# Block one's gates and branch projections turned token-major, and the last gate superblock moved ahead of the queries

## The chip, the core and the metric

One core of a Trainium2 chip runs the whole program once. The metric is device microseconds of that launch, lower is better. The core has a matrix engine (TensorE, PE in the rows, with its weight loads as PEld), VectorE (DVE), ScalarE (ACT), GpSimdE (POOL) and the queue engine SyncE (SP) that issues most DMAs.

## What is computed

Two transformer blocks over 256 tokens of width 2048, all in float32. The change lies in the first block, in this part of it:

```python
mod = (c @ w_mod + b_mod).reshape(B, 6, D)           # six rows of 2048
h = rms_norm(x, g_pre_mix) * (1 + scale_m) + shift_m
proj = h @ w_in                                       # uv, q latent, k, v, index, two gates of 2048
y_a = gmlp_spatial_gating(proj[uv], ...)              # 256 x 1024
y_b = dsa_attention(q, k, v, ...)                     # 256 x 1024, 8 heads, top-64 keys by an indexer
gates = sigmoid(proj[gate])
merged = gates[..., :D] * (y_a @ w_proj_a) + gates[..., D:] * (y_b @ w_proj_b)
x = x + gate_m * rms_norm(merged @ w_out, g_post_mix)
```

A feed-forward block and a second block (pooling, then dilated attention) follow.

## The kernel before

**Arithmetic.** Every matmul is made of three: each operand is split into a high part rounded for TensorE and a low rest, and high by high, high by low and low by high are summed in PSUM. Weights stream from HBM in pieces of 1 MB (one "call", 4 chunks of 128 rows by 512 columns). `stream_` (lines 126 to 136) loads a piece into one of 3 `raw` buffers and splits it in two halves: ScalarE writes `wh` (L134), VectorE writes `wl` (L135), 3 buffers each.

**Three ways to multiply a superblock of 512 output columns.** `lin` (L149, its matmuls L144 to L146) holds the weights still, 128 columns at a time, and moves the 256 tokens past them: 12 matmuls of 256 columns for a chunk of 128 rows. The result has features on the partitions. `linA` (L174, L192 to L194) and `linT` (L197, L211 to L213) hold 128 tokens still and move the 512 weight columns: 6 matmuls of 512 columns for the same chunk. The result has tokens on the partitions. The last chunk group of `linT` is run token half by token half, so that the first bank is done early; its `mid` is called after the first group.

**Where the low parts lie.** The program shifts the start of a low tile by 32 columns or not. The operands of the later `linT` stages (F, Y, Z) are made with the argument 0, and `xo`, which `linT` reads, with `[:, 32:]`; the operands of `lin` stages (A, K, Q, `ybl`, `yal`) are made with 32, and block one's own `xl` without a shift. K feeds both `lin` (keys) and `linA` (values).

**Order of block one.** `start` normalises the input and runs the first three quarters of rows of the eleven superblocks 0 to 10 of `w_in` (0 q latent; 1, 2 the token-major z; 3, 4 u; 5, 6 keys; 7, 8 token-major values; 9, 10 the first half of the first gate), setting partial sums aside in SBUF. Then jobs follow in the order of the string ORDER: `m` finishes uv, `G2` and `G3` are whole superblocks of the first gate (`gate_all`, 16 chunks), `g9 g10` finish the two begun ones, `k`, `v` keys and values, `S` the spatial gating (`gmlp`, mostly VectorE), `Q` the queries with their rotation (L350 to L352), `A` starts the attention, and `p0` to `p3` multiply y_a by `w_pa` (`proj`, L624: gate times projection into `mrg`). The last loop (L664) takes four superblocks of the second gate (`w_in_g2`) with y_b times `w_pb`, adds into `mrg`, and 16 splits (L680) make the operand `xh`, `xo` of the output projection (`w_out`, by `linT`).

**Side work.** At each weight piece, `side` (L520) emits `rate` tiles of `w_mod` (0.5 MB each, buffers `rawm`, accumulated on VectorE at L460; 96 of them, flushed to `mods` by 16 small matmuls at L442 every 16 tiles) and `pace` steps of a generator. The commands `r3` and `r4` in ORDER set the rate; it is 0 before. After `A` the generator is `attn1` (L1018), one step for one head: scores (L1024) to PSUM, mask, maximum, exponent, scaling, three transposes (L1054), value product (L1030 to L1032), copy into `yb` (L1033). When all heads are out, `yb` is split in two halves of four heads into `ybh` and `ybl` (L336, L337), which the second gate's `w_pb` stage reads. The framework then orders each engine's queue once, by priority and readiness; weight streams have a higher priority.

Of the kernel before, what the change touches and what calls it, by code (L numbers as in the profile page):

```python
# [10 lines left out]
F32R = mybir.dt.float32r  # L11
AF = mybir.ActivationFunctionType
ALU = mybir.AluOpType
# [3 lines left out]
P = 128  # L17
T = 256
D = 2048
KC = D // P  # L20
TX = T + 2
# [7 lines left out]
SCALE = 128.0 ** -0.5  # L29


ORDER = "m2 m3 m4 G2 g9 g10 k0 k1 v7 v8 S r3 Q A r4 p0 p1 p2 G3 p3"

PACE = (3, 1)

# [25 lines left out]
def view(tile, k, t):  # L61

    return tile[:, :k * t].rearrange("p (k t) -> p k t", k=k)
# [26 lines left out]
class Kern:  # L90
# [380 lines left out]
    def block1(self, c1):  # L471
        nc, tc, A = self.nc, self.tc, self.A
        p1 = c1.enter_context(tc.tile_pool(name="p1", bufs=1))
        xh = view(p1.tile([P, KC * TX], F32R, name="xh", tag="xh", bufs=1), KC, T)

        low = lambda i, name, dtype=F32R, t=T, pool=p1: view(
            pool.tile([P, 4 * TX + 56], dtype, name="%s%d" % (name, i), tag="xl%d" % i, bufs=1), 4, t)
        xs = [low(i, "x", F32) for i in range(4)]
        xl = {}
        X = lambda k: (xh[:, k], xl[k // 4][:, k % 4])  # L480
# [6 lines left out]
            if a >= NKEPT:  # L487
                self.cst[k] = cst[:, a - NKEPT:b - NKEPT]
        X8 = lambda name: self.cp.tile([P, 8, T], F32, name=name, tag="x", bufs=2)
        mrg = Halves([X8("mrg0"), None])  # L490
        ql = p1.tile([P, 1024], F32, name="ql", tag="ws", bufs=1)

        sbs = [(False, [ql[:, 0:512], ql[:, 512:1024]])]
# [1 line left out]
        sbs += [(False, [flat(u, 2 * s), flat(u, 2 * s + 1)]) for s in range(2)]  # L495
        sbs += [(False, [flat(kT, 2 * s), flat(kT, 2 * s + 1)]) for s in range(2)]
        sbs += [(True, [v[:, h, s * 512:(s + 1) * 512] for h in range(2)]) for s in range(2)]
        sbs += [(False, [mrg.flat(4 * s), mrg.flat(4 * s + 2)]) for s in range(2)]

# [6 lines left out]
        p1e, p1 = p1, c1.enter_context(tc.tile_pool(name="p1r", bufs=1))  # L506
# [23 lines left out]
        def finish():  # L530
            for _ in self.work:
                pass
# [4 lines left out]
            return (self.linA if tok else self.lin)(A["w_in"], n, X, 4, 4, 512, banks=self.reload(src), k0=12)  # L537

        YH = lambda name: self.place(2, name, F32R, 0)
        YL = lambda name: self.place(3, name, F32R, 32)  # L540
        qlh = p1.tile([P, 4, T], F32R, name="qlh")
        qll = view(p1.tile([P, 1088], F32R, name="qll")[:, 32:], 4, T)
        ssq = self.stat_new()
        for i, bank in enumerate(last(0)):
            for q in range(2):
                k = 2 * i + q
# [39 lines left out]
        for s in range(2):  # L586
            for i, bank in enumerate(self.lin(A["w_qidx"], s, QX, 4, 4, 512)):
                a = self.sp.tile([P, 512], F32, name="qa", tag="sw", bufs=3)
                b = self.sp.tile([P, 512], F32, name="qb", tag="th", bufs=2)
# [13 lines left out]
                nc.scalar.activation(dst, bank, AF.Tanh, scale=0.5)  # L603

        def gate_all(s):
            if mrg.tiles[1] is None:
                mrg.tiles[1] = X8("mrg1")
            for i, bank in enumerate(self.lin(A["w_in"], 9 + s, X, KC, 4, 512)):
                nc.scalar.activation(mrg.flat(4 * s + 2 * i), bank, AF.Tanh, scale=0.5)

        def keys(s):
            dst = sbs[5 + s][1]
# [6 lines left out]
                nc.scalar.copy(dst, bank)  # L619

        def proj(s):
            for i, bank in enumerate(self.lin(A["w_pa"], s, YA, 8, 4, 512)):
                m = mrg.flat(4 * s + 2 * i)
                nc.vector.scalar_tensor_tensor(m, m, 1.0, bank, ALU.add, ALU.mult)  # L624

        ya = []
        YA = lambda k: (ya[0][:, k], ya[1][:, k])

        def spatial():
# [3 lines left out]
            finish()  # L633
            ya.extend([YH("yah"), YL("yal")])
            self.gmlp(p1, u, z, *ya)
# [22 lines left out]
        finish()  # L658
        ybh, ybl = YH("ybh"), YL("ybl")
        YB = lambda k: (ybh[:, k], ybl[:, k])  # L660
        for i in range(2):
            b4 = lambda t: t[:, 4 * i:4 * i + 4]
            self.split(b4(ybh), b4(ybl), b4(yb))
        for s in range(4):  # L664
            gt = []
            for bank in self.lin(A["w_in_g2"], s, X, KC, 4, 512):
                g = self.sp.tile([P, 512], F32, name="gt", tag="gt", bufs=2)
                nc.scalar.activation(g, bank, AF.Tanh, scale=0.5)
                gt.append(g)
            for i, bank in enumerate(self.lin(A["w_pb"], s, YB, 8, 4, 512)):  # L670
                t = self.sp.tile([P, 512], F32, name="mt", tag="th", bufs=2)
                nc.vector.scalar_tensor_tensor(t, gt[i], 1.0, bank, ALU.add, ALU.mult)
                m = mrg.flat(4 * s + 2 * i)
                nc.vector.tensor_add(m, m, t)

        xo = [view(p1e.tile([P, 4 * TX + 56], F32R, name="xo%d" % i, tag="xl%d" % i, bufs=1)[:, 32:], 4, T)
              for i in range(4)]
# [41 lines left out]
        for h in range(2):  # L719
            update(h)  # L720
            self.rsum(r, ss, h)
            for c in range(4):

                m = mix[h][:, c * 512:(c + 1) * 512]
                nc.scalar.activation(m, self.xt[h][:, c * 512:(c + 1) * 512], AF.Copy, scale=r[:, h:h + 1])
                if c < 2:
                    bank = self.acc("b")
# [3 lines left out]
                    for b in range(4):  # L731
                        s = slice(b * P, (b + 1) * P)
                        modulated(4 * c + b, slice(h * P, (h + 1) * P), bank[:, s], tmp[:, s])
        for k in range(8, KC, 2):
            bank = self.acc("b")
            tmp = self.sp.tile([P, 512], F32, name="tm", tag="th", bufs=2)
            for b in range(2):
# [3 lines left out]
                s = slice(b * T, (b + 1) * T)  # L741
# [731 lines left out]
```

## Time and profile before

| | |
|---|---|
| median of 3 runs | 2440.88 us (2440.26 to 2445.6) |
| the profiled execution | 2438.1 us, of which its span in the profile 2436.1 us |
| TensorE busy | 2378.1 us, 98% of the span |
| VectorE, ScalarE busy | 1678.5 us (69%), 1246.7 us (51%) |
| DMA | 540.61 MB, mean 222 GB/s |

Busy shares are means over very different stages. Read the stage that the change touches (about 240 to 690 us) by windows of time, and take durations there from start to start of successive instructions, since matmuls overlap.

### The profile page before, as it was taken

To read this page: it belongs to the slowest core of one execution; us is meant where nothing else is said; L and a number is where in the kernel's file an instruction comes from. 1 tells how busy PE (TensorE), PEld (TensorE's weight loads), DVE (VectorE), ACT (ScalarE), POOL (GpSimd) and SP (SyncE) were. 2 spreads that over 40 slices of the span, in tenths; PEclk is the share of its full clock that TensorE was granted. 3 is DMA by queue.
4 is the path that set the end of the run, shared out by engine and by line. 5 is a ranking of instruction groups with operands and counts; after the bars stand their busy time and mean duration, and the time that the engine had idled before them with its cause. 6 is when DMAs were issued, how large, how long until landed. Compare 5 with 4: busy or idle time off the path is not lost.

```text
span 2436.1 us, 37172 instructions
## 1 busy us (share of the span) xinstructions
PE 2378.1 (98%) x15142; PEld 2153.9 (88%) x15142; DVE 1678.5 (69%) x2213; ACT 1246.7 (51%) x1716; POOL 19.3 (1%) x30
## 2 busy tenths in 40 slices
PE   7999999999989999999999989999999999999997
PEld 6899989999868888888888879998898899999986
DVE  8997898888777575555556566756664477777764
ACT  5877674534464444444445454445644455554543
POOL 0000000000000000000000000000000000000000
PEclk9999999999999999999999999999999999999999
DMA  9997557999948585555555545555655544454453
GB/s 365 349 365 259 182 177 272 329 350 333 350 161 321 191 291 193 190 189 187 194 197 200 190 149 191 191 189 186 228 193 190 190 163 167 158 189 169 161 190 138
DMA packets 104043, 540.61 MB, mean 222 GB/s; under 512 B 9888, under 2 KB 18240, under 8 KB 53184
## 3 DMA queue, kind: packets, MB, share of 16 engines
q1 hardware_dynamic: 100896, 526.19, 60.8%
q10 hardware_dynamic: 2160, 8.88, 1.0%
q0 software_dynamic: 816, 3.16, 0.4%
q8 instruction: 118, 1.93, 0.3%
q14 instruction: 53, 0.43, 0.1%
HBM read 533.99 MB, written 4.21 MB: 221 GB/s over the span
## 4 chain that ended last, share of the span: by engine, by line
PE 94%; DVE 2%; ACT 1%; DMA 1%; issue 1%; POOL 0%; SPq 0%; DVEq 0%; POOLq 0%
PE acca L145 15%; PE acca L144 15%; PE acca L146 15%; PE acca L212 11%; PE acca L211 11%; PE acca L213 11%; PE acca L193 2%; PE acca L194 2%; PE acca L192 2%; PE accb L212 2%; PE accb L213 2%; PE accb L211 2%; DMA hid<-in_w_mod_dram 1%; DVE wl L135 1%; PE accb L1343 1%
## 5 line engine op out<-in xcount | busy, mean ns | idle before, releaser
L135 DVE TENSOR_TENSOR wl<-raw,wh 128x1024 fp32r<-128x1024 f32 x802 | 977.9, 1221 | 570.9 <-ACT wh L134 568.3
L134 ACT CAST wh<-raw 128x1024 fp32r<-128x1024 f32 x802 | 841.7, 1051 | 864.0 <-PE acca L213 377.9
L145 PE MATMUL acca<-Ql,wh 128*128 128x256 f32 x1024 | 290.5, 284 | 0.0
L144 PE MATMUL acca<-Qh,wh 128*128 128x256 f32 x1024 | 289.8, 284 | 0.0
L146 PE MATMUL acca<-Qh,wl 128*128 128x256 f32 x1024 | 285.5, 281 | 0.0
L212 PE MATMUL acca<-wl,Fh 128*128 128x512 f32 x704 | 276.8, 393 | 1.0 <-DVE wl L135 0.9
L213 PE MATMUL acca<-wh,Fl 128*128 128x512 f32 x704 | 275.7, 393 | 0.3 <-DVE Fl L716 0.3
L211 PE MATMUL acca<-wh,Fh 128*128 128x512 f32 x704 | 252.3, 396 | 1.7 <-ACT Fh L714 1.7
L144 PE MATMUL acca<-xh,wh 128*128 128x256 f32 x832 | 232.8, 284 | 4.5 <-ACT xh L808 3.4
L145 PE MATMUL acca<-xl,wh 128*128 128x256 f32 x832 | 233.7, 284 | 0.0
L146 PE MATMUL acca<-xh,wl 128*128 128x256 f32 x832 | 227.0, 283 | 0.0
L144 PEld LDWEIGHTS acca<-Qh,wh 128*128 128x128 f32 x1024 | 192.9, 188 | 0.5
L145 PEld LDWEIGHTS acca<-Ql,wh 128*128 128x128 f32 x1024 | 192.6, 188 | 0.8
L146 PEld LDWEIGHTS acca<-Qh,wl 128*128 128x128 f32 x1024 | 192.1, 189 | 0.4
L144 PEld LDWEIGHTS acca<-xh,wh 128*128 128x128 f32 x832 | 158.1, 190 | 7.3 <-ACT xh L808 3.6
L145 PEld LDWEIGHTS acca<-xl,wh 128*128 128x128 f32 x832 | 157.4, 189 | 1.6 <-issue 0.7
L212 PEld LDWEIGHTS acca<-wl,Fh 128*128 128x128 f32 x704 | 132.7, 189 | 29.1 <-DVE wl L135 2.2
L211 PEld LDWEIGHTS acca<-wh,Fh 128*128 128x128 f32 x704 | 131.3, 188 | 30.0 <-ACT Fh L714 2.9
L213 PEld LDWEIGHTS acca<-wh,Fl 128*128 128x128 f32 x704 | 132.4, 188 | 28.6 <-DVE Fl L716 1.5
L146 PEld LDWEIGHTS acca<-xh,wl 128*128 128x128 f32 x832 | 155.1, 190 | 1.3 <-issue 1.0
L145 PE MATMUL acca<-Al,wh 128*128 128x256 f32 x512 | 143.7, 282 | 0.0
L144 PE MATMUL acca<-Ah,wh 128*128 128x256 f32 x512 | 142.7, 281 | 0.0
(374 smaller groups left out, 4600.5 us busy)
## 6 DMA issues: line engine op xcount, KB each, us to landing
raw<-in_w_fgu_dram SPq DMA_DIRECT2D x88, 1024.0 KB, 4.8
raw<-in_w_inb_dram SPq DMA_DIRECT2D x64, 1024.0 KB, 4.8
raw<-in_w_in_dram SPq DMA_DIRECT2D x51, 1024.0 KB, 6.3
rawm<-in_w_mod_dram SPq DMA_DIRECT2D x96, 512.0 KB, 5.7
raw<-in_w_fd_dram SPq DMA_DIRECT2D x44, 1024.0 KB, 4.8
raw<-in_w_ina_dram SPq DMA_DIRECT2D x32, 1024.0 KB, 4.8
raws<-in_w_mod_dram SPq DMA_DIRECT2D x30, 1024.0 KB, 8.4
raw<-in_w_in_g_dram SPq DMA_DIRECT2D x16, 1024.0 KB, 7.2
```

Source lines behind the costliest of these rows:

```text
L134: nc.scalar.copy(wh[:, :per], raw[:, a:a + per])
L135: nc.vector.tensor_sub(wl[:, :per], raw[:, a:a + per], wh[:, :per].bitcast(F32))
L144: mm(out, ah, bh, start=start, stop=False, skip_group_check=True)
L145: mm(out, ah, bl, start=False, stop=False, skip_group_check=True)
L146: mm(out, al, bh, start=False, stop=stop, skip_group_check=True)
L192: mm(banks[h], xh[:, t], wh[:, s], start=fresh and k == 0, stop=False, skip_group_check=True)
L193: mm(banks[h], xh[:, t], wl[:, s], start=False, stop=False, skip_group_check=True)
L194: mm(banks[h], xl[:, t], wh[:, s], start=False, stop=k == nk - 1, skip_group_check=True)
L211: mm(banks[h][q], xh[:, t], wh[:, w], start=k == 0, stop=False, skip_group_check=True)
L212: mm(banks[h][q], xh[:, t], wl[:, w], start=False, stop=False, skip_group_check=True)
L213: mm(banks[h][q], xl[:, t], wh[:, w], start=False, stop=k == nk - 1, skip_group_check=True)
L1343: nc.tensor.matmul(ps[:, g * T:(g + 1) * T], q[g][:, P:T], kT, start=g == 0, stop=g == 1, skip_group_check=True)
```

## The change

Superblocks 9 and 10 (both their begun and their last part), `G2`, `G3`, the four `p` projections, and the second gate with its `w_pb` products go from `lin` to the token-major `linA` and `linT`. `mrg` becomes two token-half tiles of 2048 columns, both reserved at the start. The operand of the output projection has to be feature-major, so `turn` transposes `mrg` on TensorE, two chunks at a time, and splits from PSUM: six turns inside the last `w_pb` superblock (for the columns of the first three), two behind it. The low tiles `xs`, `xl` move by 32 columns, `yal`/`ybl` change their shift. In ORDER, `G3` goes from between `p2` and `p3` to between `S` and `r3 Q`.

```diff
-ORDER = "m2 m3 m4 G2 g9 g10 k0 k1 v7 v8 S r3 Q A r4 p0 p1 p2 G3 p3"
+ORDER = "m2 m3 m4 G2 g9 g10 k0 k1 v7 v8 S G3 r3 Q A r4 p0 p1 p2 p3"
...
-            pool.tile([P, 4 * TX + 56], dtype, name="%s%d" % (name, i), tag="xl%d" % i, bufs=1), 4, t)
+            pool.tile([P, 4 * TX + 56], dtype, name="%s%d" % (name, i), tag="xl%d" % i, bufs=1)[:, 32:], 4, t)
...
-        mrg = Halves([X8("mrg0"), None])
+        mrg = [X8("mrg%d" % h).rearrange("p a t -> p (a t)") for h in range(2)]
...
-        sbs += [(False, [mrg.flat(4 * s), mrg.flat(4 * s + 2)]) for s in range(2)]
+        sbs += [(True, [m[:, s * 512:(s + 1) * 512] for m in mrg]) for s in range(2)]
...
-        YL = lambda name: self.place(3, name, F32R, 32)
+        YL = lambda name: self.place(3, name, F32R, 0)
...
         def gate_all(s):
...
-            for i, bank in enumerate(self.lin(A["w_in"], 9 + s, X, KC, 4, 512)):
-                nc.scalar.activation(mrg.flat(4 * s + 2 * i), bank, AF.Tanh, scale=0.5)
+            for m, bank in zip(mrg, self.linT(A["w_in"], 9 + s, X, KC, 4, 512)):
+                nc.scalar.activation(m[:, s * 512:(s + 1) * 512], bank[0], AF.Tanh, scale=0.5)
...
         def proj(s):
-            for i, bank in enumerate(self.lin(A["w_pa"], s, YA, 8, 4, 512)):
...
+            for m, bank in zip(mrg, self.linT(A["w_pa"], s, YA, 8, 4, 512)):
...
+        def turn(k):
+            bank = self.acc("b")
+            for b in range(2):
+                for h in range(2):
+                    nc.tensor.transpose(bank[:, b * T + h * P:b * T + (h + 1) * P],
+                                        mrg[h][:, (k + b) * P:(k + b + 1) * P], self.ident)
+            self.split(xh[:, k:k + 2], xo[k // 4][:, k % 4:k % 4 + 2], bank.rearrange("p (b t) -> p b t", b=2), 0.5)
+
         for s in range(4):
             gt = []
-            for bank in self.lin(A["w_in_g2"], s, X, KC, 4, 512):
+            for bank in self.linT(A["w_in_g2"], s, X, KC, 4, 512):
...
-            for i, bank in enumerate(self.lin(A["w_pb"], s, YB, 8, 4, 512)):
+            turned = lambda: [turn(k) for k in (range(0, 12, 2) if s == 3 else ())]
+            banks = self.linT(A["w_pb"], s, YB, 8, 4, 512, mid=turned)
...
+        for k in range(12, 16, 2):
+            turn(k)
         XO = lambda k: (xh[:, k], xo[k // 4][:, k % 4])
-        for k in range(KC):
-            self.split(*XO(k), mrg(k), 0.5)
```

## Rows read from the trace of the kernel before

**Rows 1.** The page: busy time by engine, the chain's shares, the weight split's group.
```profile
PE 2378.1 (98%) x15142; PEld 2153.9 (88%) x15142; DVE 1678.5 (69%) x2213; ACT 1246.7 (51%) x1716; POOL 19.3 (1%) x30
...
PE 94%; DVE 2%; ACT 1%; DMA 1%; issue 1%; POOL 0%; SPq 0%; DVEq 0%; POOLq 0%
...
L135 DVE TENSOR_TENSOR wl<-raw,wh 128x1024 fp32r<-128x1024 f32 x802 | 977.9, 1221 | 570.9 <-ACT wh L134 568.3
```

**Rows 2.** Windows of 20 us: window, length, engines' busy time, PE clock, DMA.
```profile
340.00:360.00 20.00, 20.00 (x141) 18.57 (x140) 19.32 (x35) 13.43 (x21) 0.00 (x0) 1.00 0.47 168
...
500.00:520.00 20.00, 20.00 (x171) 20.00 (x171) 14.99 (x14) 8.45 (x9) 0.00 (x0) 1.00 0.96 352
...
600.00:620.00 20.00, 20.00 (x99) 16.85 (x98) 14.83 (x18) 8.67 (x13) 0.66 (x1) 1.00 0.95 360
```

**Rows 3.** Windows of 1 us in the gap, same columns.
```profile
363.00:364.00 1.00, 0.00 (x0) 0.00 (x0) 1.00 (x2) 1.00 (x2) 0.00 (x0) 1.00 0.81 246
...
367.00:368.00 1.00, 0.00 (x0) 0.00 (x0) 1.00 (x2) 0.53 (x1) 0.00 (x0) 0.53 0.99 377
...
373.00:374.00 1.00, 1.00 (x7) 1.00 (x7) 1.00 (x3) 0.99 (x2) 0.00 (x0) 0.56 0.81 115
```

**Rows 4.** Waits between 330 and 380 us: total us, times, longest.
```profile
PE acca L144 <- DVE qT L350: 6.7, 1, 6.7
```

**Rows 5.** Timeline of PE, a `lin` stage (second gate): start, duration.
```profile
500.49 0.28 PE L144 MATMUL acca<-xh,wh 128*128 128x256 f32 x1
...
507.93 0.28 PE L144 MATMUL acca<-xh,wh 128*128 128x256 f32 x1
```

**Rows 6.** Timeline of PE, a `linT` stage (output projection).
```profile
640.36 0.39 PE L211 MATMUL acca<-wh,xh 128*128 128x512 f32 x1
...
645.80 0.39 PE L211 MATMUL acca<-wh,xh 128*128 128x512 f32 x1
```

**Rows 7.** Timeline of PE, a `linA` stage (values of block two, operand K).
```profile
1860.88 0.39 PE L192 MATMUL acca<-wh,Kh 128*128 128x512 f32 x1
...
1866.43 0.39 PE L192 MATMUL acca<-wh,Kh 128*128 128x512 f32 x1
```

**Rows 8.** Timeline of PE, transposes between matmuls of a `linT` stage.
```profile
1706.63 0.39 PE L213 MATMUL acca<-wh,Yl 128*128 128x512 f32 x1
1706.87 0.38 PE L241 MATMUL accb<-cst,x 128*128 128x128 f32 x2
1707.00 0.48 PE L211 MATMUL acca<-wh,Yh 128*128 128x512 f32 x1
1707.32 0.81 PE L241 MATMUL accb<-cst,x 128*128 128x128 f32 x6
1707.89 0.47 PE L212 MATMUL acca<-wl,Yh 128*128 128x512 f32 x1
1708.20 0.39 PE L213 MATMUL acca<-wh,Yl 128*128 128x512 f32 x1
```

**Rows 9.** Timeline of PE, steps of the attention heads 1, 6, 7 and 8.
```profile
388.65 0.27 PE L1054 MATMUL accb<-cst,e 128*128 128x128 f32 x1
...
441.26 0.27 PE L1054 MATMUL accb<-cst,e 128*128 128x128 f32 x1
...
447.86 0.90 PE L1024 MATMUL accb<-kT,qT 128*128 128x128 f32 x4
...
454.33 0.27 PE L1054 MATMUL accb<-cst,e 128*128 128x128 f32 x1
...
468.19 0.27 PE L1054 MATMUL accb<-cst,e 128*128 128x128 f32 x1
```

**Rows 10.** Instructions by tile: count, duration min/median/max, first and last start.
```profile
L144 PE MATMUL acca<-yah,wh x128: 274/280/551, 369.4 to 453.0; 128*128 128x256 f32 x128
...
L337 DVE TENSOR_TENSOR ybl<-yb,ybh x2: 1211/1214/1218, 458.5 to 474.4; 128x1024 fp32r<-128x1024 f32 x2
...
L144 PE MATMUL acca<-ybh,wh x128: 274/282/367, 478.8 to 595.8; 128*128 128x256 f32 x128
```

More of the change, by code (lines that the diff above doesn't have):

```diff
@@ L605, in gate_all @@
         def gate_all(s):
-            if mrg.tiles[1] is None:
-                mrg.tiles[1] = X8("mrg1")
-            for i, bank in enumerate(self.lin(A["w_in"], 9 + s, X, KC, 4, 512)):
-                nc.scalar.activation(mrg.flat(4 * s + 2 * i), bank, AF.Tanh, scale=0.5)
+            for m, bank in zip(mrg, self.linT(A["w_in"], 9 + s, X, KC, 4, 512)):
+                nc.scalar.activation(m[:, s * 512:(s + 1) * 512], bank[0], AF.Tanh, scale=0.5)
         def keys(s):
@@ L621, in proj @@
         def proj(s):
-            for i, bank in enumerate(self.lin(A["w_pa"], s, YA, 8, 4, 512)):
-                m = mrg.flat(4 * s + 2 * i)
-                nc.vector.scalar_tensor_tensor(m, m, 1.0, bank, ALU.add, ALU.mult)
+            for m, bank in zip(mrg, self.linT(A["w_pa"], s, YA, 8, 4, 512)):
+                m = m[:, s * 512:(s + 1) * 512]
+                nc.vector.scalar_tensor_tensor(m, m, 1.0, bank[0], ALU.add, ALU.mult)
         ya = []
@@ L663, in block1 @@
             self.split(b4(ybh), b4(ybl), b4(yb))
+        def turn(k):
[5 more added lines that the diff above has]
+            self.split(xh[:, k:k + 2], xo[k // 4][:, k % 4:k % 4 + 2], bank.rearrange("p (b t) -> p b t", b=2), 0.5)
         for s in range(4):
             gt = []
-            for bank in self.lin(A["w_in_g2"], s, X, KC, 4, 512):
+            for bank in self.linT(A["w_in_g2"], s, X, KC, 4, 512):
                 g = self.sp.tile([P, 512], F32, name="gt", tag="gt", bufs=2)
-                nc.scalar.activation(g, bank, AF.Tanh, scale=0.5)
+                nc.scalar.activation(g, bank[0], AF.Tanh, scale=0.5)
                 gt.append(g)
-            for i, bank in enumerate(self.lin(A["w_pb"], s, YB, 8, 4, 512)):
+            if s == 3:
+                xo = [view(p1e.tile([P, 4 * TX + 56], F32R, name="xo%d" % i, tag="xl%d" % i, bufs=1)[:, 32:], 4, T)
+                      for i in range(4)]
+            turned = lambda: [turn(k) for k in (range(0, 12, 2) if s == 3 else ())]
+            banks = self.linT(A["w_pb"], s, YB, 8, 4, 512, mid=turned)
+            for h, (m, bank) in enumerate(zip(mrg, banks)):
                 t = self.sp.tile([P, 512], F32, name="mt", tag="th", bufs=2)
-                nc.vector.scalar_tensor_tensor(t, gt[i], 1.0, bank, ALU.add, ALU.mult)
-                m = mrg.flat(4 * s + 2 * i)
+                nc.vector.scalar_tensor_tensor(t, gt[h], 1.0, bank[0], ALU.add, ALU.mult)
+                m = m[:, s * 512:(s + 1) * 512]
                 nc.vector.tensor_add(m, m, t)
-        xo = [view(p1e.tile([P, 4 * TX + 56], F32R, name="xo%d" % i, tag="xl%d" % i, bufs=1)[:, 32:], 4, T)
-              for i in range(4)]
+        for k in range(12, 16, 2):
+            turn(k)
         XO = lambda k: (xh[:, k], xo[k // 4][:, k % 4])
-        for k in range(KC):
-            self.split(*XO(k), mrg(k), 0.5)
         if todo and todo[0][0] < 48:
```

## The prediction

> **What bounds the kernel now.** I read the page first. TensorE is busy for 98% of the span and holds 94% of the chain that ended last [rows 1]. So the time is TensorE's work plus its few holes, and an edit pays only where it shortens TensorE's stream or fills a hole. Windows of time come next. Where the change is, TensorE is full, with VectorE at 15 us or more of 20 and, later on, the DMA share at 0.95 [rows 2]. The exception is a hole from 362.7 us on: VectorE is busy all the time, TensorE does nothing, and its clock, 2.4 GHz until then, drops to half (1.2 GHz) at about 367.5 us and comes back at about 373.6 us [rows 3]. The waits name what ended it: the first matmul of `p0` waited 6.7 us for VectorE's rotation of the last queries, which had to free a PSUM bank [rows 4]. VectorE is not slow at one thing there; it works off a queue (spatial gating, top-k, key rotation, weight splits). Last, the timelines give the pitch of each kind of matmul and the progress of the attention heads.
>
> **The change part by part.**
>
> *Fewer, longer matmuls.* What is converted: superblocks 9 and 10 (2 x 192 matmuls of 256 columns), G2 and G3 (2 x 192), four projections (4 x 96), second gate (4 x 192), `w_pb` (4 x 96), together 2304, which become 1152 of 512 columns. In `lin`, the 63 matmuls between the two rows take 7.44 us, 118.1 ns each [rows 5]. In `linT`, 24 take 5.44 us, 226.7 ns each [rows 6]. So 2304 x 0.1181 = 272.1 us become 1152 x 0.2267 = 261.2 us: **-10.9 us**. The two rows together say 0.424 ns a column and 9.5 ns a matmul whatever its length; the columns stay the same and 1152 fixed parts go. `linA` with an operand shifted by 32 takes 5.55 us for 24, 231.3 ns [rows 7]; at that price the gain would be 272.1 - 266.5 = 5.6 us, the lower bound. I take the upper one, because the new operands have the arrangement of the output projection's `xh`, `xo`, whose row is the 226.7.
>
> The Trainium skill (TensorE: Matmul & The Clock Gate, "Back-to-back issue gap") prices a warm matmul at N / 2.4 + 2.5 ns, hence a fixed part of 2.5 ns. By it this edit would be worth 1152 x 2.5 = 2.9 us, an estimate from that page, and the whole sum below would be near nothing. The rows differ from it (109.2 against a measured 118.1, 215.8 against 226.7), so the rows decide.
>
> *Shifted low parts.* z and v already run by `linA` (384 matmuls), at the shift that is slow for it; they should gain 231.3 - 226.7 = 4.6 ns each, -1.8 us. The `lin` stages that stay (q latent, u, keys, index: 1008 matmuls) get the other shift. No row shows `lin` so. The nearest is `linA`, which loses 4.6 ns a matmul at the shift that isn't its own; I bound the loss by nothing (the shift may not matter to `lin`) and by that, 0 to +4.6 us, and take the middle, +2.5. Together **+0.7**.
>
> *Turns.* 32 transposes are new. Eight of them and three matmuls of `linT` take 1.57 us [rows 8], less 3 x 0.227 leaves 0.111 us each: **+3.6 us** of TensorE, which nothing hides since TensorE is the bound. The 16 splits of L680 become 8 larger ones; they lie on ScalarE and VectorE behind TensorE's work. Behind the last `w_pb` matmul two turns wait for VectorE's two evictions; the first 12 chunks of the output projection, 72 x 0.2267 = 16.3 us, cover them. I put +0.5 (bounds 0 and +2).
>
> The skill's same page ("Part 4: PE-mode transpose") has about 275 ns for a transpose within a kernel; by that the 32 would cost 8.8 us, an estimate, and the sum would be 5.2 us worse. The rows show less than half of it, since transposes overlap the matmuls beside them.
>
> *G3 ahead of the queries.* G3 is 96 x 0.2267 = 21.8 us of TensorE that needs nothing of the spatial gating. Placed after S it stands in front of the queries in TensorE's queue; four 1 MB loads pass the queries' loads in SP's queue, where the DMA share is 0.47 [rows 2], and 8 splits of 1.22 us [rows 1], 9.8 us, pass the queue on VectorE, 8 casts and two tanh that on ScalarE (13.4 of 20 us busy). VectorE so wins 21.8 - 9.8 = 12 us on TensorE, and it was 6.7 us late. The hole closes: -6.7 us, and with it the half clock from 369.4 to 373.6 us, 4.2 us of work at half speed, -2.1: **-8.8** (bound above: nothing, if the queue only moves).
>
> *What G3 covered where it was.* Between the first `p0` matmul (369.4) and the first that reads `ybh` (478.8) lie 109.4 us [rows 10]. In them eight heads go by, one behind the other: the next head's scores come with the transposes of the one before, 388.65 to 468.19 is 79.5 us for seven steps, 11.4 us a head, although a step can take 6.5 us (447.86 to 454.33) [rows 9]. The split of the second half of `yb` ends at 474.4 + 1.2 = 475.6, 3.2 us before it is wanted [rows 10]. So that cover is nearly used up already. After the change it is 109.4 less G3 (22.7), less the projections' and the gate's own gain (576 x 0.1181 - 288 x 0.2267 = 2.7), less the half clock (2.1), = 81.9; the first four chunks of `w_pb` read only the first half of `yb` and add 24 x 0.2267 = 5.4: 87.3 us. The heads need 475.6 - 369.4 - 2.1 = 104.1 at the old pace: TensorE would stand for 16.8 us, queued behind its first matmul on heads 5 to 8, with the second gate's next superblocks behind it; an idle stretch of that kind cost another 2.1 of half clock above. That is the upper bound, +18.9. Against it: the last step took 13.9 us (454.33 to 468.19), and with TensorE idle it can take 6.5, which leaves 9.4; between heads 6 and 7 the row of 6.6 us (441.26 to 447.86) goes to a flush of `mods` that waited for its tiles, and these come sooner with 4 MB of G3's weights out of the way, which leaves down to 2.8. The lower bound is nothing. I take 4 and 2 for the clock: **+6**.
>
> *DMA.* The `mods` tiles share the queue with the weights; at 500 us it moves 352 GB/s, and the highest of these rows is 360 [rows 2]. If as many tiles go with each piece, 4% faster pieces want 366. I put **+1** (bounds 0 and +4).
>
> Sum: -10.9 + 0.7 + 3.6 + 0.5 - 8.8 + 6 + 1 = **-7.9 us**, from the profiled execution's 2438.1 (span 2436.1 and 2.0 around it) to 2430.2. The median of the runs lies 2.8 above the profiled one, so I expect a median of about **2433**.
>
> **The rivals.**
>
> *Attention is covered after all* (the queue is ordered anew, and heads get through at 9 us): the +6 falls away, -13.9, 2427. For it: steps of 6.5 us exist. Against it: the mean is 11.4.
>
> *Attention keeps its pace*, and the hole moves from 362 us to the first `w_pb`: +18.9 instead of +6, sum +5.0, 2446, slower. For it: only 3.2 us of slack in the rows, and 22.7 us of cover taken away. The change is slower once that stall with its clock costs over 13.9 us.
>
> *A matmul costs by its columns alone, or what its count saves is lost* to the unshifted `lin` stages and to DMA: the terms -10.9, +0.7 and +1 become 0, sum +1.3, 2442. For it: DMA at 0.95. Against it: the output projection runs at 226.7 ns under the same DMA load. The back-to-back rule of the skill's TensorE page would put the time close to here.
>
> *The hole doesn't close*, because VectorE's queue and not the lack of matmuls sets when `p0` can start: -8.8 becomes 0, sum +0.9, 2442. Against it stand the 12 us that VectorE wins.
>
> **How the numbers follow.** A measurement of this kernel tells 0.2%, 4.9 us, from no change: faster means under 2436.0, slower over 2445.8. Chances: the forecast 0.45, with its own range of 2428 to 2438; attention covered 0.22; attention at the old pace 0.13; no gain from the count 0.12; hole not closed 0.08. Three quarters of the forecast's case and all of the second are faster: 0.34 + 0.22 = 0.56. Slower is two thirds of the third case and a little of the last two: 0.11. The rest, 0.33, is within. The range 2425 to 2444 leaves out a little below and most of the third case above.
>
> **What would show it.** Matmuls of the gates at about 227 ns start to start; z and v at 227, u and keys between 118 and 122. No wait on `qT` at the first `p0` matmul, and no half clock near 370 us. A wait of 3 to 10 us at the second chunk group of the first `w_pb` superblock, ended by the second half's split; it is the step I trust least. Transposes near 0.11 us, none ahead of an idle TensorE. The prediction is wrong if that wait is over 14 us, if the old hole stands, or if `lin` loses more than 5 ns a matmul.

## The result and the profile after

The changed kernel takes 2460.43 us (median of 4 runs, 2458.24 to 2463.15), the kernel before 2441.93 beside it (4 runs, 2440.26 to 2445.6): a ratio of 1.0076, interval 1.0064 to 1.0088. It is 18.5 us slower; the forecast was 2433. The profiled execution took 2459.31 us, span 2456.9 against 2436.1.

The page after, busy time and the chain, for [rows 1]: TensorE is busy for 3.9 us more than before, with 1120 instructions fewer, because some of them run at half clock (the windows below). Its share of the chain fell from 94% to 88%; DMA, at 1% before, has 4%.
```profile
PE 2382.0 (97%) x14022; PEld 2106.2 (86%) x14022; DVE 1678.9 (68%) x2205; ACT 1245.4 (51%) x1708; POOL 18.5 (1%) x30
...
PE 88%; DMA 4%; DVE 4%; ACT 2%; issue 1%; POOL 0%; SPq 0%; DVEq 0%; ACTq 0%; POOLq 0%
```
Where the time came and went, by tile (count, durations, first and last start), for [rows 10]:
```profile
L211 PE MATMUL acca<-wh,yah x64: 388/389/579, 380.2 to 432.4; 128*128 128x512 f32 x64
...
L337 DVE TENSOR_TENSOR ybl<-yb,ybh x2: 1216/1216/1217, 453.7 to 490.2; 128x1024 fp32r<-128x1024 f32 x2
...
L211 PE MATMUL acca<-wh,ybh x64: 389/389/397, 458.2 to 590.9; 128*128 128x512 f32 x64
...
L213 PE MATMUL acca<-wh,xo x128: 388/389/474, 615.2 to 706.5; 128*128 128x512 f32 x128
```
The last of these lines before:
```profile
L213 PE MATMUL acca<-wh,xo x128: 387/389/398, 596.3 to 686.2; 128*128 128x512 f32 x128
```
TensorE starts the first `w_pb` 20.6 us earlier than before (458.2 against 478.8, [rows 10]), ends the last one only 4.9 earlier (590.9 against 595.8), and starts on `xo` 18.9 later (615.2 against 596.3). So TensorE was early at `w_pb`; 15.7 us of its lead went between first and last `w_pb`, and 23.8 us between the last `w_pb` and the output projection. Some 5 of the 15.7 are no loss: the last four heads' own matmuls, which lay ahead of `w_pb` before, lie inside it now (an estimate from the starts in the timeline). From there on nothing changes: the last `xo` matmul is 20.3 later, the span 20.8 longer.

The second loss is one wait, the longest of TensorE (total us, times, longest). The wait of [rows 4] is gone:
```profile
PE accb L442 <- DVE rawm L460: 15.3, 1, 15.3
...
PE acca L212 <- DVE wl L135: 6.3, 4, 2.2
```
The timeline of TensorE there: the last `w_pb` matmul, the fifth flush of `mods` (L442), and behind it the turn's transposes (L667):
```profile
591.32 0.39 PE L213 MATMUL acca<-wh,ybl 128*128 128x512 f32 x1
606.99 3.54 PE L442 MATMUL accb<-cst,rawm 128*128 128x1 f32 x16 [15.28 <-DVE rawm L460]
610.39 3.65 PE L667 MATMUL accb<-cst,mrg 128*128 128x128 f32 x16
```
And the chain over the same stretch (start, us, what): the loads of the last `w_mod` tiles and their sums, one behind the other.
```profile
591.85 1.29 DVE mac L460
...
593.16 6.61 DMA rawm<-in_w_mod_dram
...
599.86 1.30 DVE mac L460
...
601.17 4.29 DMA rawm<-in_w_mod_dram
...
605.55 1.30 DVE rawm L460
...
606.99 3.56 PE accb L442 x16
```
The operand `xh`, `xo` is made by the turns, so the output projection waits for them, and they wait for a flush that needs 16 summed tiles. Both take their PSUM tile from the pool "b", which, by the program, hands its four out in the order in which they are asked for; the flush was emitted first. All 32 transposes came behind it, also those of the six turns that were meant for the inside of the last `w_pb` superblock. Two views of the tile sums show the other half of it. In the kernel before, the group sums (`rawm` as result, one for each 16 tiles) of the window from 380 to 470 us and from 440 to 660 us:
```profile
L460 DVE SCALAR_TENSOR_TENSOR rawm<-rawm,vec,mac x2: 1276/1278/1279, 388.5 to 443.0; 128x1024 f32<-128x1024 f32 x2
...
L460 DVE SCALAR_TENSOR_TENSOR rawm<-rawm,vec,mac x4: 1276/1278/1282, 443.0 to 607.2; 128x1024 f32<-128x1024 f32 x4
```
After:
```profile
L460 DVE SCALAR_TENSOR_TENSOR rawm<-rawm,vec,mac x2: 1275/1276/1278, 411.8 to 462.8; 128x1024 f32<-128x1024 f32 x2
...
L460 DVE SCALAR_TENSOR_TENSOR rawm<-rawm,vec,mac x4: 1274/1278/1284, 462.8 to 605.6; 128x1024 f32<-128x1024 f32 x4
```
The second group is 19.8 us later than before, because `r3` stands behind G3 now. From there the tiles came faster than before (48 tiles in 142.8 us, before 164.2), and the fifth group ended about when it did (605.6, before 607.2). TensorE was early, the tiles were not. Before, the fifth flush had its place behind some 70 matmuls of the output projection, and TensorE waited for nothing there.

The first loss, around the first `w_pb`, in windows of 40 us (columns as in [rows 2]; the second window is that of the other loss). Before:
```profile
460.00:500.00 40.00, 40.00 (x342) 40.00 (x340) 37.53 (x37) 18.37 (x24) 0.00 (x0) 1.00 0.94 346
580.00:620.00 40.00, 40.00 (x252) 36.10 (x251) 32.15 (x36) 17.60 (x24) 0.66 (x1) 1.00 0.96 371
```
After:
```profile
460.00:500.00 40.00, 35.02 (x157) 27.56 (x155) 31.28 (x39) 17.91 (x35) 0.00 (x0) 0.91 0.87 307
580.00:620.00 40.00, 24.72 (x119) 21.52 (x118) 31.52 (x32) 11.25 (x16) 0.00 (x0) 0.79 0.83 294
```
The second half of `yb` is split only at 490.2. TensorE does the first half of the first `w_pb`; next in its queue comes the second gate's next superblock, and it finds no weights split for that. In part this is VectorE, where `wl` stands behind tile sums and the heads' steps. VectorE's timeline (start, duration; TensorE waited 2.24 us for the last line):
```profile
475.49 1.28 DVE L460 SCALAR_TENSOR_TENSOR mac<-rawm,vec,mac 128x1024 f32<-128x1024 f32 x1 [1.09 <-DMA rawm<-in_w_mod_dram]
476.69 0.55 DVE L1036 SCALAR_TENSOR_TENSOR e<-accb,sc 128x384 f32<-128x384 f32 x1
477.15 1.27 DVE L460 SCALAR_TENSOR_TENSOR mac<-rawm,vec,mac 128x1024 f32<-128x1024 f32 x1
478.35 0.60 DVE L1052 TENSOR_REDUCE mx<-e 128x1 f32<-128x128 f32 x2
478.87 1.27 DVE L460 SCALAR_TENSOR_TENSOR mac<-rawm,vec,mac 128x1024 f32<-128x1024 f32 x1
480.06 1.21 DVE L135 TENSOR_TENSOR wl<-raw,wh 128x1024 fp32r<-128x1024 f32 x1
```
In part it is the buffers. There are three for split weights; the first `w_pb`'s second half, cast by then, holds two of them until the heads are done, so the gate superblock goes through one. ScalarE's casts show it: each starts when the last matmul of the piece before it ends (these start at 471.61, 476.83, 484.90 and 489.90 and take 0.4 us).
```profile
472.09 1.04 ACT L134 CAST wh<-raw 128x1024 fp32r<-128x1024 f32 x1 [0.91 <-PE acca L213]
...
477.26 1.05 ACT L134 CAST wh<-raw 128x1024 fp32r<-128x1024 f32 x1 [1.84 <-DVE e L1036]
...
485.33 1.04 ACT L134 CAST wh<-raw 128x1024 fp32r<-128x1024 f32 x1 [3.14 <-PE acca L213]
...
490.33 1.05 ACT L134 CAST wh<-raw 128x1024 fp32r<-128x1024 f32 x1 [1.00 <-PE acca L213]
```
This is read from the trace; no run changes the number of buffers.

### The profile page after: what moved, and what is told of

Same layout as the page of the kernel before. It is cut to its first block, busy times and chain, and to the rows that moved or that the text cites. A ratio compares the mean times of both kernels' runs of the same rounds, so it can differ in the third digit from the quotient of the medians.

```text
span 2456.9 us, 34876 instructions
## 1 busy us (share of the span) xinstructions
PE 2382.0 (97%) x14022; PEld 2106.2 (86%) x14022; DVE 1678.9 (68%) x2205; ACT 1245.4 (51%) x1708; POOL 18.5 (1%) x30
## 4 chain that ended last, share of the span: by engine, by line
PE 88%; DMA 4%; DVE 4%; ACT 2%; issue 1%; POOL 0%; SPq 0%; DVEq 0%; ACTq 0%; POOLq 0%
PE acca L212 13%; PE acca L213 13%; PE acca L211 13%; PE acca L145 11%; PE acca L144 11%; PE acca L146 11%; PE acca L193 2%; PE acca L194 2%; PE acca L192 2%; DMA rawm<-in_w_mod_dram 2%; PE accb L212 2%; PE accb L211 2%; PE accb L213 2%; DMA hid<-in_w_mod_dram 1%; DVE wl L135 1%
## 5 line engine op out<-in xcount | busy, mean ns | idle before, releaser
L146 PE MATMUL acca<-Ah,wl 128*128 128x256 f32 x512 | 140.8, 280 | 0.0
L212 PE MATMUL acca<-wl,xh 128*128 128x512 f32 x320 | 128.7, 402 | 5.8 <-DVE wl L135 5.8
L460 DVE SCALAR_TENSOR_TENSOR mac<-rawm,vec,mac 128x1024 f32<-128x1024 f32 x84 | 107.4, 1279 | 27.7 <-DMA rawm<-in_w_mod_dram 27.4
L211 PE MATMUL acca<-wh,xh 128*128 128x512 f32 x320 | 117.1, 398 | 2.0 <-ACT wh L134 2.0
L144 PEld LDWEIGHTS acca<-Ah,wh 128*128 128x128 f32 x512 | 96.5, 189 | 0.0
L144 PE MATMUL acca<-xh,wh 128*128 128x256 f32 x320 | 91.8, 291 | 4.7 <-ACT xh L817 3.5
```

The lines of the kernel that those rows point to most:

```text
L144: mm(out, ah, bh, start=start, stop=False, skip_group_check=True)
L146: mm(out, al, bh, start=False, stop=stop, skip_group_check=True)
L211: mm(banks[h][q], xh[:, t], wh[:, w], start=k == 0, stop=False, skip_group_check=True)
L212: mm(banks[h][q], xh[:, t], wl[:, w], start=False, stop=False, skip_group_check=True)
L460: nc.vector.scalar_tensor_tensor(dst, raw, cc, self.mac, ALU.mult, ALU.add)
```

## The experiments

Theory A was: the `w_mod` tiles are a second chain beside TensorE, and everything that stands behind one of their flushes waits for them. Rivals were that the loss hangs on the new form of the matmuls, on the heads alone, or on VectorE. "Busy" in the table is TensorE's busy time with its mean clock in the windows 460 to 500 and 580 to 620 us of the profiled execution; ratios are to runs of the kernel before taken beside each run (their medians lie between 2441.85 and 2442.59). "Flush 5" is the start of the fifth flush of `mods`.

| run | median us | ratio to before | busy, clock 460:500 | busy, clock 580:620 | flush 5 at |
|---|---|---|---|---|---|
| before | 2441.93 | | 40.0, 1.00 | 40.0, 1.00 | 612.4 |
| after | 2460.43 | 1.0064 to 1.0088 | 35.0, .91 | 24.7, .79 | 607.0 |
| e1_turn_bank_a | 2445.72 | 1.0002 to 1.0021 | 34.9, .96 | 35.7, .91 | 608.2 |
| e2_g3_old_place | 2450.66 | 1.0019 to 1.0045 | 36.0, .96 | 38.4, .96 | 599.4 |
| e3_move_alone | 2455.87 | 1.0040 to 1.0070 | 35.7, .96 | 40.0, 1.00 | 631.5 |
| e4_rate_2 | 2451.03 | 1.0021 to 1.0043 | 35.5, 1.00 | 34.3, .87 | 654.5 |
| e5_tiles_with_g3 | 2441.36 | 0.9984 to 1.0003 | 33.5, .92 | 40.0, 1.00 | 581.3 |
| e6 (e5, other pool) | 2449.74 | 1.0020 to 1.0039 | 34.0, .96 | 35.9, .91 | 577.9 |
| e7 (e2, other pool) | 2451.38 | 1.0026 to 1.0052 | 36.2, .96 | 37.1, .91 | 598.5 |
| e8 (e3, early tiles) | 2452.51 | 1.0030 to 1.0061 | 34.1, .91 | 40.0, 1.00 | 595.7 |
| e9_half_loads | 2441.17 | 0.9985 to 1.0003 | 35.6, .91 | 38.1, 1.00 | 587.7 |
| e10 (before, half loads) | 2443.29 | 0.9995 to 1.0014 | 40.0, 1.00 | 40.0, 1.00 | 579.6 |
| e11_half_sums | 2452.83 | 1.0028 to 1.0061 | 37.6, 1.00 | 21.2, .74 | 597.4 |
| e12 (e2, half loads) | 2441.62 | 0.9988 to 1.0006 | 38.5, 1.00 | 39.8, 1.00 | 573.7 |
| e13 (half loads and sums) | 2439.24 | 0.9977 to 0.9996 | 35.6, .96 | 40.0, 1.00 | 563.6 |
| e14 (before, half both) | 2446.83 | 1.0011 to 1.0029 | 37.4, .96 | 40.0, 1.00 | 553.9 |
| e16_sums_off_vector | 2535.85 | 1.0365 to 1.0396 | 33.8, .96 | 36.1, 1.00 | 667.1 |
| e17 (e16, early tiles) | 2518.33 | 1.0292 to 1.0323 | 37.1, .96 | 35.7, 1.00 | 646.8 |
| e23_half_loads_no_heads_needed | 2447.37 | 1.0007 to 1.0025 | 40.0, 1.00 | 27.1, .74 | 592.9 |
| e25_tiles_with_g3_gate_ahead | 2440.47 | 0.9989 to 1.0006 | 38.0, 1.00 | 36.8, 1.00 | 589.0 |

**The flush in front of the turn.** e1 gives the turn the other PSUM pool, and nothing else.
```
-            bank = self.acc("b")
+            bank = self.acc("a")
```


> The changed kernel, but the transposes write to banks of the other PSUM pool (the matmul accumulators'), so that they no longer take their turn behind the fifth mods flush. Theory A (the transposes queue in their pool behind a flush whose w_mod tiles are late): the hole of 15 us after the last w_pb superblock goes, with its half clock and slow start; the stretch from the last w_pb matmul to the last w_out matmul was 115 us, is 94 to 95 by its matmuls, and some 4 us of wait for the flush stay: about 17 us less than the changed kernel, 2443 us. Rival B (the loss is the moved G3, at the first w_pb): under 3 us less, 2457 or more. Rival C (w_mod's bytes alone bind, whoever waits for them): about 5 us less, 2455.

2445.72: 14.7 us of the 18.5 are gone, as A said. The flush comes no sooner (608.2), but now TensorE waits 0.7 us for it:
```profile
PE acca L667 <- DVE xo L340: 2.5, 2, 1.4
...
PE accb L442 <- DVE rawm L460: 0.7, 1, 0.7
```
The pool has a price of its own, the 2.5 us on the turn's splits; by the program, two of its four tiles hold the sums of `w_pb`.

**The parts alone.** e2 is the changed kernel with the old ORDER, e3 the kernel before with the new one.
```
e2: ORDER = "... v7 v8 S r3 Q A r4 p0 p1 p2 G3 p3"
e3: ORDER = "... v7 v8 S G3 r3 Q A r4 p0 p1 p2 p3"
```


> The changed kernel with G3 back between p2 and p3: the token-major part alone. Theory A: the transposes still stand behind the fifth flush, and its last tile came at 606 us in both kernels, so a hole of 15 to 20 us stays at the end of the last w_pb; the old hole at 362 us is back; about 2452 us. Rival B: all of the loss is gone, 2436 us. Rival C: as much time for the tiles as before, so no loss either, 2438 us.

> The kernel before with nothing but the new ORDER: the move alone, feature-major, no transposes. Theory A: no hole at the last w_pb, since its splits take no PSUM bank; the hole at 362 us closes (-8.8 us) and one of 6 to 9 us opens at the first w_pb: 2442 us, give or take 3. Rival B: most of the loss is here, 2455 us or more. Rival C: the flushes come late here too and stand ahead of w_out's matmuls, about 2450 us.

Both lose, 2450.66 and 2455.87. e2 came out as A had it in total, but by luck: A had a hole of 15 to 20 us before the flush, and TensorE stands only 1.6 us there; 4.0 us of idle and some clock lie in the window 460 to 500, where the kernel before lost nothing. e3 refutes A's 2442, and by its number B was right: the move costs without any turn. Its chain shows a tile's load at another place, an eviction of the output projection (`mix`) on VectorE behind a tile's load, for which TensorE waits 11.7 us:
```profile
642.16 1.29 DVE mac L460
...
643.47 7.38 DMA rawm<-in_w_mod_dram
...
650.94 1.21 DVE mac L460
652.15 0.68 DVE mix L930
...
652.97 0.77 PE acca L211
```

**The tiles' time.** e4 sets `r2` for `r4`; e5 moves one word.
```
e4: ORDER = "... v7 v8 S G3 r3 Q A r2 p0 p1 p2 p3"
e5: ORDER = "... v7 v8 S r3 G3 Q A r4 p0 p1 p2 p3"
```


> The changed kernel with r2 in place of r4: half as many w_mod tiles are emitted with a piece of weights, so the flush that stands ahead of the transposes is the fourth (64 tiles) and not the fifth (80). The same pool and the same queueing. Theory A: the fourth flush's tiles were in at 565 us in the changed kernel, before the transposes want the bank, so the hole shrinks to under 4 us: 2443 us. Rival B: no change, 2460 us. Rival C: no change in bytes, so at most 5 us less.

> The changed kernel with one word moved: the rate for the w_mod tiles is set ahead of the moved gate superblock instead of behind it, so the tiles start about 20 us sooner against TensorE's work. Theory A (the tiles are paced by their own loads and sums, 3.2 us each; the late start puts flush 5 under the last branch projection and the last heads behind flush 2): the hole of 15.3 us at 591.7 goes, the loss around the first branch projection falls from about 15 to under 10 us, and the time is 2440 us, between 2436 and 2446. Theory B (the time is lost because the heads lie one superblock later against TensorE's work, whatever the tiles do): 2455 or more. Theory C (tiles that start sooner take the DMA queues and VectorE from the moved gate itself): a new hole of 5 us or more between 345 and 390 us, and 2446 to 2454.

e4 misses (2451.03): at half the rate it is the fourth flush that lies before the turn, 5.7 us late, and TensorE stands 15.2 us from 691.4 on, before the sixth, where the changed kernel stands 7.6 us between the output projection and the next stage. (The profile ends this wait with a norm's sum on VectorE, not with a tile.) e5 gives A's time, 2441.36, and refutes B's 2455: G3 is where the change put it, and 19.1 us are back. Its flush 5 is at 581.3, now ahead of the last `w_pb` superblock in TensorE's queue, and the second window is full. A's other half missed: the first loss, which should have fallen, is 6.5 us of idle between 460 and 520 us, in the changed kernel 6.4. The windows of e5:
```profile
460.00:500.00 40.00, 33.47 (x155) 26.58 (x154) 31.49 (x38) 18.34 (x37) 0.00 (x0) 0.92 0.84 303
580.00:620.00 40.00, 40.00 (x203) 33.70 (x202) 34.03 (x36) 18.69 (x24) 1.77 (x3) 1.00 0.90 332
```
It pays elsewhere too: all sixteen tiles of the first group are pulled forward to before 259 us (in the changed kernel eight, and the next not before 387), into the index stage, where TensorE stands 2.8 us and runs 6.8 us at half clock; the spatial gating starts 5.4 us later than in the changed kernel (348.9 against 343.5).

e6 and e7 are e5 and e2 with the turn in the other pool, e8 is e3 with `r3 G3`.

> As the run before it, and the turn's transposes take their PSUM tiles from the other pool. Theory A: with the tiles early enough the fifth flush no longer stands in the turn's way, so the pool matters by less than 4 us: 2438, between 2434 and 2444. If the pool alone were the cause, the two runs would still differ by 10 us or more, as 2460 and 2446 did.

> Token-major gates and projections with the gate superblock at its old place, and the turn's transposes in the other pool: the one half of the change without its wait. Theory A: 2450.7 of the run with the old place, less 1.6 us of hole and some 5 us of half clock before the turn: 2444, between 2440 and 2448; the hole of 7 us behind the spatial gating stays. If the token-major form by itself costs nothing beyond that (the working of the forecast had -10.9 for the count, +0.7 for the shifted low parts and +4.1 for the turns), it would be 2436.

> The kernel before, with the gate superblock moved alone, and the rate for the w_mod tiles set ahead of it. Theory A: the late tiles were what cost the move alone its 13 us against the kernel before, so the 11.7 us hole at 641 and its half clock go, the hole behind the spatial gating stays closed, and the time is 2438, between 2434 and 2444. Theory B (heads later, tiles without part in it): 2452 or more.

Three misses. With the other pool, e6 is 8 us slower than e5 by the medians (3 by the profiled spans) and has 4 us of waits on VectorE at the transposes; e7 is 0.7 from e2. The other pool pays only where a flush is late. In e8 the hole at 641 is gone as expected, but in its profiled execution the spatial gating starts 10 us later (356.8, in e3 346.6), and by the medians only 3 of the 13 us come back: by its number B was right here too. Between 240 and 720 us TensorE waits 14 us for weight splits in it (e3: 5.7); what early tiles have to do with that isn't settled.

**Bytes or VectorE.** In e9, e10 and e12, 14 of 16 tiles of a group load half their columns and sum that half twice; a sum takes 1281 ns, in the kernel before 1279.
```
+        if 0 < k < KC - 1:
+            nc.sync.dma_start(raw[:, :4 * P], self.A["w_mod"][k * P:(k + 1) * P, at * P:(at + 4) * P])
+            two = lambda t: t.rearrange("p (a n) -> p a n", a=2)
+            nc.vector.scalar_tensor_tensor(two(self.mac), raw[:, None, :4 * P].to_broadcast([P, 2, 4 * P]), cc,
+                                           two(self.mac), ALU.mult, ALU.add)
+            return
```


> The changed kernel, in which 14 of the 16 w_mod tiles of each group load only half of their columns (0.25 instead of 0.5 MB) and sum that half twice, so VectorE's instructions stay as they are and the mods come out as those of other weights. Theory D (the stretch from 380 to 660 us, with a DMA share of 0.82 to 0.99, is fed too slowly for a TensorE that is 20 us ahead and 4% faster; late tiles and late wl are two faces of it): the loss of 14 to 16 us between 460 and 512 falls under 5, the hole of 15.3 us before flush 5 goes with its half clock, and the time is 2432, between 2426 and 2438. Theory V (VectorE's instructions are the bound, not the bytes): 2455 or more. Theory H (the heads are late whatever the tiles do): only the end hole goes, 2440 to 2446.

> The kernel before with the same half loads of the w_mod tiles, as the control. TensorE was busy there all through the stretch, and the hole behind the spatial gating doesn't hang on the tiles. Theory D: within 4 us of the kernel before, 2441, hole of 6.7 us kept. If DMA had cost the kernel before something too, it would be 2436 or less.

> Token-major form with the gate superblock at its old place and the half loads of the w_mod tiles. Theory D: the 10 us that the form alone loses between 460 and 540, and the 2 to 6 before its last flush, were want of bytes; they go, and what is left is the forecast's own sum for the form (-10.9 + 0.7 + 4.1 = -6 us): 2437, between 2432 and 2442. If the form itself is dear (its order of loads, its waits on wl), 2446 or more.

In e11 they load all and sum half.
```
+        if 0 < k < KC - 1:
+            m = self.mac[:, :4 * P]
+            nc.vector.scalar_tensor_tensor(m, raw[:, :4 * P], cc, m, ALU.mult, ALU.add)
+            return
```


> The changed kernel with full loads, in which 14 of the 16 w_mod tiles of each group sum only half of their columns: the bytes stay, VectorE's 1.3 us of a tile falls to some 0.7 (the mods come out wrong in half of their columns). Theory D (bytes): the tiles come no sooner, 2455 to 2461. Theory V (VectorE): 2430 to 2442. If both share it, because loads wait for their buffers until VectorE has read them: in between, 2443 to 2454.

Half the bytes bring the changed kernel to 2441.17, the kernel before (e10) stays where it was, and e12 is 9 us under e2. In e9 the fifth flush has the place in TensorE's queue that it had, behind the last `w_pb` and ahead of the turns, and TensorE does not wait there: in the changed kernel the end hole was want of bytes, as Theory D has it. But e9's first window is nearly as empty as the changed kernel's, and D's 2432 did not come. Both, the time and the windows, are what Theory H had (2440 to 2446, only the end hole gone). In e12 the framework's order is another as well: the fifth flush stands behind 144 of the 192 matmuls of `w_pb`, in e2 behind all, so its 9 us aren't shown to be the bytes alone. Half sums (e11, 2452.83, in the range that was put for a shared cause) shrink the first loss and keep the second, 16.3 us on L442:
```profile
460.00:500.00 40.00, 37.60 (x181) 30.71 (x182) 28.45 (x39) 18.65 (x31) 0.00 (x0) 1.00 0.88 318
580.00:620.00 40.00, 21.21 (x104) 18.07 (x102) 22.67 (x33) 9.95 (x14) 1.76 (x3) 0.74 0.83 299
```
e13 (changed kernel) and e14 (kernel before) load and sum half.

> The changed kernel in which 14 of the 16 w_mod tiles of each group load and sum only half of their columns (the mods come out wrong in half of their columns). If the hole before flush 5 is want of bytes (it went with half loads) and the loss around the first branch projection is VectorE's queue (10.5 us with half loads, 4.5 with half sums), then both go: 2441 of the half loads less some 6, 2435, between 2430 and 2439. If the heads themselves are late, whatever VectorE has beside them: 2440 to 2445.

> The kernel before with the same half loads and half sums, as the control: its TensorE was busy through the stretch with all bytes and all sums, so 2442, between 2438 and 2445. The difference of this run to the one before it is what the change is worth with VectorE and DMA out of its way: the forecast had -7.9, and -13.9 with attention covered.

Together they give 2439.24, just above what I expected, and the first window doesn't fill (35.6 of 40). The control e14 is slower than the kernel before, with less work: shorter sums also change the order into which the framework puts each queue, and new waits on `wl` appear in it (2.6 us at 463.7, 2.4 at 530.0). So e11, e13 and e14 don't settle what VectorE's sums are worth, and the 7.6 us between e13 and e14 are no measure of the change.

e16 and e17 leave nothing out; ScalarE scales a tile, GpSimd adds it.
```
-            nc.vector.scalar_tensor_tensor(dst, raw, cc, self.mac, ALU.mult, ALU.add)
+            nc.scalar.mul(raw, raw, cc)
+            nc.gpsimd.tensor_tensor(dst, self.mac, raw, ALU.add)
```


> The changed kernel, nothing left out, in which ScalarE scales each w_mod tile in place and GpSimd adds it to the sum, so that VectorE loses 1.28 us a tile. If VectorE's queue makes the loss around the first branch projection and bytes make the end hole, the first shrinks to under 5 and the second stays (10 to 17 us): 2452, between 2446 and 2457, as with half sums. If a sum on GpSimd takes longer than the 3.2 us between tiles, tiles come later still: 2460 or more.

> The same with the rate set ahead of the moved gate superblock, so that the tiles start sooner; nothing left out. That version took 2441 with 12 us lost around the first branch projection. If those are VectorE's queue: 2434, between 2429 and 2439, faster than both kernels. If ScalarE or GpSimd becomes the bound or holds VectorE up: 2443 or more.

Both much slower. The waits of e16 between 380 and 640 us say why: now it is ScalarE that stands on the loads, with the casts `wh` queued behind, and VectorE and TensorE behind those. And its tiles come later still: the largest single loss is again the fifth flush ahead of the turns, 38.8 us (last line, from TensorE's timeline), more than half of the 75 us that e16 lies over the changed kernel. In e17, whose tiles start sooner, that wait is gone, and it is still 77 us over e5.
```profile
ACT rawm L460 <- DMA rawm<-in_w_mod_dram: 74.9, 30, 5.8
DVE wl L135 <- ACT wh L134: 43.8, 27, 5.8
...
PE acca L212 <- DVE wl L135: 18.1, 27, 3.1
...
667.15 3.57 PE L442 MATMUL accb<-cst,rawm 128*128 128x1 f32 x16 [38.76 <-POOL rawm L461]
```
**The heads.** e23 is e9, in which the first superblock of `w_pb` multiplies `X` in place of `YB`.
```
-            banks = self.linT(A["w_pb"], s, YB, 8, 4, 512, mid=turned)
+            banks = self.linT(A["w_pb"], s, YB if s else X, 8, 4, 512, mid=turned)
```


> The changed kernel with the half loads of the w_mod tiles (14 of 16 tiles of a group load 0.25 MB and sum it twice), in which the first superblock of the second branch projection also multiplies the normed input instead of the heads' output: TensorE needs nothing of the heads before the second superblock. Against 2441 of the half loads alone. Theory H (the heads, late against TensorE, are what it stands for): of the 10.5 us lost between 460 and 500 under 4 stay, 2434, between 2430 and 2437. Theory V (wl behind VectorE's sums): the loss stays, 2439 to 2444.

Its windows; e9's are in the table:
```profile
460.00:500.00 40.00, 40.00 (x202) 33.76 (x201) 33.88 (x43) 21.26 (x39) 0.00 (x0) 1.00 0.74 247
580.00:620.00 40.00, 27.07 (x126) 23.52 (x127) 34.60 (x37) 11.31 (x16) 1.76 (x3) 0.74 0.69 240
```
The first loss is gone. The edit takes away only TensorE's need of the heads; tile loads and sums are those of e9. So the loss hangs on that need, as Theory H has it, though not as a wait of TensorE on the heads: in e9 its waits between 380 and 640 us are on weight splits (`wh` 2.5 us, `wl` 2.2), with the casts one by one as above (472.2, 477.6, 485.1, 490.6). (The framework's order of the queues shifts somewhat here too.) Yet the time rises to 2447.37. TensorE comes to the fifth flush earlier and stands there 13.5 us; the flush is at 592.9, no sooner than in e9 (587.7). The window came out as H said and the time did not: what is won at the heads is lost at the tiles.

e25 leaves nothing out: e5, with the second gate computed one superblock ahead of `w_pb` (and buffers for its result).
```
+        ahead = gate2(0)
         for s in range(4):
+            gt, ahead = ahead, gate2(s + 1) if s < 3 else None
```


> Nothing left out: the changed kernel with the rate set ahead of the moved gate superblock (2441), in which the second gate runs one superblock ahead of the branch projection, so that the heads have 21.8 us more of TensorE's work to hide behind. Theory H: the 12 us around the first branch projection fall under 4, 2433, between 2429 and 2437, faster than both kernels. Theory V: they stay, only a few us later, 2438 to 2444.

2440.47, not the 2433 of H: the first window loses 2.0 us instead of 6.5 and its clock stays up, but 2.6 us of idle follow between 500 and 520, and 3.2 appear in the second window, where the flush is at 589.0 (e5: 581.3). It is not told apart from the kernel before. None of the versions with the full work is faster than the kernel before.

## Why the prediction was wrong

**Right.** *Fewer, longer matmuls.* G3's matmuls, for [rows 6]: 24 in 5.45 us, 227.1 ns, against the 226.7 used. *Turns*: eight transposes between 617.62 and 618.41 are under 0.1 us each (0.111 used). *The hole closes*: first `yah` matmul 10.8 us later with 21.8 us of G3 ahead of it, so 11.0 won, 8.8 and a bit of the count's gain forecast; the granted clock is 1.00 from 350 to 390 us. *`lin` at the other shift*: 73 matmuls of the keys, whose low operand `xl` was moved, take 8.75 us, 119.9 ns, +1.8 against 118.1 [rows 5]; +2.5 us had been put in, 1008 x 0.0018 = 1.8 is what this row makes of it. In e2 the keys have 119.9 too; in e3, where nothing is shifted, `lin` has 118.3 there. The timeline of TensorE after, for these:
```profile
325.07 0.28 PE L144 MATMUL acca<-xh,wh 128*128 128x256 f32 x1
...
333.82 0.28 PE L146 MATMUL acca<-xh,wl 128*128 128x256 f32 x1
...
354.76 0.62 PE L211 MATMUL acca<-wh,xh 128*128 128x512 f32 x2
...
360.21 0.62 PE L211 MATMUL acca<-wh,xh 128*128 128x512 f32 x2
...
617.62 1.03 PE L667 MATMUL accb<-cst,mrg 128*128 128x128 f32 x8
...
618.41 0.47 PE L213 MATMUL acca<-wh,xo 128*128 128x512 f32 x1
```
The Trainium skill (TensorE: Matmul & The Clock Gate, "Back-to-back issue gap") has, for an isolated warm matmul, a gap of 518 cycles at 512 columns, 215.8 ns at 2.4 GHz; the trace does not agree, with 227.1 here and 226.7 before.

**The step that failed** is the term for the turns, +0.5 with bounds 0 and +2: "Behind the last `w_pb` matmul two turns wait for VectorE's two evictions". It took the turns for free of everything else. They share a PSUM pool with the flushes, and all eight stood behind the fifth: +0.5 became 15.3 us of idle, and half clock (granted 0.50) until 614.1, another 3.6 on the 7.1 us of work behind it. The prediction had read such a wait itself, 6.6 us between two heads that went to a flush, and did not carry it over to the turns.

With it failed the sentence on the `mods` tiles: "these come sooner with 4 MB of G3's weights out of the way". I counted the bytes that left and not the command that starts the tiles. `r3` is behind G3 in the new order; the second group ended 19.8 us later, and the fifth no sooner than 605.6. e1 (the pool alone, -14.7) and e5 (the tiles alone, -19.1) show both halves: either takes the long wait away, and neither brings the 2433.

***What G3 covered* (+6) was too small.** From the first `yah` matmul to the split of the second half the heads take 490.2 - 380.2 = 110.0 us, before 474.4 - 369.4 = 105.0. They caught up nothing, as the rival "attention keeps its pace" had it. Between 460 and 510 us TensorE idles 6.4 us, where 4 were put in, and its granted clock in five windows of 10 us is 0.87, 0.96, 0.83, 1.00 and 0.83, which makes at most 5 us where 2 were put in (an estimate: half of the 10 us at half clock): some 11 in all, under the bound of 18.9. The mechanism was another than forecast: no wait for the second half's split came at the second chunk group. The queue has the next gate superblock there, and TensorE waits for its weights, held back by two of three buffers. The two terms together, 18.9 for 0.5 and some 11 for 6, make 23 to 24 of the 29 us by which the profiled execution missed 2430.2. e23 shows that the first of the two losses hangs on the heads, and also that filling that hole alone brings little: TensorE then stands longer at the flush.

***DMA* (+1, at most +4)** priced the bytes as a rate and not as a second chain with a start and an end. With G3 at its old place the new form is 8 us slower than the kernel before, 2450.66 against 2442.59, where the forecast's terms for the form have -6 (-10.9 + 0.7 + 4.1). With half the tiles' bytes it is -1.7 (e12 less its control e10), which their spreads don't tell from nothing. Where the other 4 us are, and what of the 9 us between e2 and e12 is bytes and what the framework's order, these runs don't settle.

**Open.** How the 11 us of the first loss divide between the held buffers, the tile sums in front of `wl` and the framework's order isn't settled: half sums change the order too, and no run has more buffers.

## What to carry to other kernels

A busy TensorE can hide a second chain that ends only a little earlier than it is needed; before making TensorE faster, list what each side chain (here tile loads, their sums, a flush) has as start, pace and due time, and look for the first thing that shares an in-order queue or a pool with it. When a word that starts a stream is passed in an order, the stream moves, not only the step. And an engine that stands on a side load holds up everything queued behind it: who stands matters more than how long the work is.

## What the runs showed of the hardware

A sum of 128 x 1024 floats took a mean of 2704 ns on GpSimd (e16; median 2409, and the profile is rough there) against 1279 ns for multiply and add on VectorE, with 1150 ns more on ScalarE for the scaling. Moving the low operand by 32 columns took `lin`'s matmuls of 256 columns from 118.1 to 119.9 ns. Less work made a kernel slower: e14, the kernel before with half loads and half sums of its tiles, took 2446.83 against 2442.42.
